# An unused tile of 96 bytes among the constants of a two-layer decoder trunk

## The chip, the cores and the metric

The kernel runs on one core of a Trainium2 chip. The metric is the device time of one execution in microseconds (us). A core has the engines TensorE (matrix products; PE in the profile, with its weight loads as PEld), VectorE (DVE), ScalarE (ACT), GpSimd (POOL) and SyncE (SP), which issues most of the transfers. The engines work on the on-chip memory of 128 partitions; an address here is a byte offset within a partition. TensorE writes its sums to a second memory, PSUM.

## What is computed

Two layers of a decoder over 256 tokens and 2048 features, in float32. Layer A's mixer is dilated attention, layer B's is a gated sum of compressed, selected-block and sliding-window attention. Cut to what matters:

```
h = x                                                   # (1, 256, 2048)
for i in range(2):
    hn = rmsnorm(h, attn_norm_g[i])
    if i == 0:
        h = h + dilated_mixture_attention(hn, a_w_in, a_w_out)
    else:
        shared = nsa_shared_kv(rmsnorm(h, kv_norm_g), w_kv_shared, ...)
        h = h + nsa_attention(hn, b_w_qg, b_w_out, *shared)
    hn = rmsnorm(h, mlp_norm_g[i])
    h = h + square(relu(hn @ mlp_w1[i])) @ mlp_w2[i]    # 2048 -> 8192 -> 2048
    gate = sigmoid(rmsnorm(h, ple_norm_g[i]) @ ple_w_gate[i])
    h = h + (p[i] @ ple_w_proj[i]) * gate
return rmsnorm(h, final_norm_g)
```

## The kernel before

Every matrix of weights is read once, in chunks of 128 x 1024 float32 (512 KB). `load` (L186) brings a chunk into a tile `raw`. ScalarE (`copy`, L198) rounds it into `whi`, a tile of type float32r, the type that TensorE multiplies at a higher rate than float32; VectorE (`sub`, L204) writes the rest, `raw - whi`, into `wlo`. Activations are split in the same way: a tile `xa` (or `h`, `oT`, `ko`, `pg`) holds the high part of 256 tokens in columns 0 to 255 and the low part in columns 256 to 511. A product is then the sum of three float32r products: high by high, high by low, low by high.

A matmul has a stationary operand of 128 x 128, which is loaded first as its weights, and a moving operand that streams past it.

- `mm_tiles` (L327, L329) does the products with the features in the partitions: 128 columns of `whi` as weights with all 512 columns of `xa` moving, then the same columns of `wlo` with the 256 columns of the high part. `quad` and `single` call it.
- `token_major` (L418, L419, L420) does the products with the tokens in the partitions: 128 columns of the activations as weights, and 512 columns of `whi` or `wlo` moving.
- The last chunk of the last gate (L382, L383, L384) uses 256 moving columns in all three products.
- Scores in layer A (L717, L718), the norms' sums (L237, L261) and the transposes (L491, L555, L746, L1180) are plain float32. The transposes have the constant `ident` as the moving operand; L261 has the constant `ones` as weights.

`Program.run` writes the order out: at each step it loads chunks up to 7 ahead, splits some, gives the active generators (the steps behind a product: sums, norms, softmax) one move each and lets TensorE work on one chunk. The work of the attention heads is hooked between chunks.

The tiles are given out pool by pool, in the order in which the pools are opened: `const`, `x`, `stat`, `tmp`, `xa`, `w`, and behind them pools that live for a stage (`A`, `h`, `O`, `B`, `C`, `S`). Within the constants the order is that of the program: `gains`, `ones`, `ident`, `ropeC`, `ropeS`, `pair`, `warm`. Each tile's size is rounded up to 32 bytes. `warm` has one float32 in each partition.

Of the kernel before, what the change touches and what calls it, by code (L numbers as in the profile page):

```python
# [10 lines left out]
F32 = mybir.dt.float32  # L11
# [4 lines left out]
P = 128  # L16
# [117 lines left out]
def kernel(ctx: ExitStack, tc: tile.TileContext, a: dict, out: bass.AP):  # L134
# [4 lines left out]
    const = ctx.enter_context(tc.tile_pool(name="const", bufs=1))  # L139
# [33 lines left out]
    ropeS = const.tile([32, T], F32, name="ropeS")  # L173
    pair = const.tile([P, 64], F32, name="pair")
    warm = const.tile([P, 1], F32, name="warm")
    nc.scalar.copy(warm, ones[:, :1])

    def load_x(j, half=None):
# [1155 lines left out]
```

## Time and profile before

| | |
|---|---|
| median of 3 runs | 2513.16 us (2512.55 to 2513.68) |
| profiled execution | 2514.11 us, its span 2511.3 us |
| mean granted TensorE clock | 0.999 |
| TensorE busy | 2500.4 us, 13497 matmuls |
| weight loads busy | 2156.5 us |
| VectorE busy | 1662.3 us |
| ScalarE busy | 1351.0 us |
| read from device memory | 461.65 MB, 185 GB/s over the span |

The span runs from the first to the last instruction of the profiled execution; the execution's own time also holds what lies around it. Busy time counts each instruction from its start to its end. Matmuls overlap, so that the duration of one (396 ns for 512 columns on L327) is longer than the distance from its start to the next one's start; the timeline shows the starts.

### The profile page before, as it was taken

To read this page: it belongs to the slowest core of one execution; us is meant where nothing else is said; L and a number is where in the kernel's file an instruction comes from. 1 tells how busy PE (TensorE), PEld (TensorE's weight loads), DVE (VectorE), ACT (ScalarE), POOL (GpSimd) and SP (SyncE) were. 2 spreads that over 40 slices of the span, in tenths; PEclk is the share of its full clock that TensorE was granted. 3 is DMA by queue.
4 is the path that set the end of the run, shared out by engine and by line. 5 is a ranking of instruction groups with operands and counts; after the bars stand their busy time and mean duration, and the time that the engine had idled before them with its cause. 6 is when DMAs were issued, how large, how long until landed. Compare 5 with 4: busy or idle time off the path is not lost.

```text
span 2511.3 us, 36082 instructions
## 1 busy us (share of the span) xinstructions
PE 2500.4 (100%) x13497; PEld 2156.5 (86%) x13497; DVE 1662.3 (66%) x2808; ACT 1351.0 (54%) x2168; POOL 10.4 (0%) x24
## 2 busy tenths in 40 slices
PE   9999999999999999999999999999999999999998
PEld 8888888888888888888888889888888888888887
DVE  7766677865465565566787989766546556556676
ACT  6444444554454453455564788755545445445455
POOL 0000000000000000000000000000000000000000
PEclk9999999999999999999999999999999999999999
DMA  7555545556555655555565753455555655665553
GB/s 272 172 179 178 175 161 181 173 188 193 193 188 193 191 192 193 192 192 185 186 195 189 243 163 121 141 191 190 192 192 188 193 192 192 193 192 190 182 189 121
DMA packets 130111, 466.10 MB, mean 186 GB/s; under 512 B 14608, under 2 KB 15888, under 8 KB 129936
## 3 DMA queue, kind: packets, MB, share of 16 engines
q1 hardware_dynamic: 129264, 462.68, 56.6%
q8 instruction: 105, 1.72, 0.3%
q0 software_dynamic: 528, 1.07, 0.2%
q14 instruction: 70, 0.57, 0.1%
q10 hardware_dynamic: 144, 0.07, 0.0%
HBM read 461.65 MB, written 2.10 MB: 185 GB/s over the span
## 4 chain that ended last, share of the span: by engine, by line
PE 99%; DVE 0%; DMA 0%; SPq 0%; ACT 0%; issue 0%; DVEq 0%
PE mm L327 22%; PE at L327 17%; PE mm L329 11%; PE at L329 9%; PE mm L418 6%; PE mm L420 6%; PE mm L419 6%; PE at L420 5%; PE at L418 5%; PE at L419 5%; PE at L1180 0%; PE at L718 0%; PE mm L1204 0%; PE mm L938 0%; PE mm L939 0%; DMA raw<-in_w_v 0%
## 5 line engine op out<-in xcount | busy, mean ns | idle before, releaser
L204 DVE TENSOR_TENSOR wlo<-raw,whi 128x1024 fp32r<-128x1024 f32 (+1 forms) x875 | 1065.7, 1219 | 634.3 <-PE at L420 131.5
L198 ACT CAST whi<-raw 128x1024 fp32r<-128x1024 f32 (+1 forms) x875 | 919.8, 1052 | 880.4 <-PE at L327 198.9
L327 PE MATMUL mm<-xa,whi 128*128 128x512 f32 x2176 | 756.4, 396 | 0.0
L329 PE MATMUL mm<-xa,wlo 128*128 128x256 f32 x2176 | 587.9, 278 | 0.0
L327 PE MATMUL at<-xa,whi 128*128 128x512 f32 x1648 | 573.7, 393 | 0.0
L327 PEld LDWEIGHTS mm<-xa,whi 128*128 128x128 f32 x2176 | 401.4, 188 | 85.1 <-issue 0.4
L329 PE MATMUL at<-xa,wlo 128*128 128x256 f32 x1648 | 458.5, 278 | 0.0
L329 PEld LDWEIGHTS mm<-xa,wlo 128*128 128x128 f32 x2176 | 409.4, 188 | 9.7
L327 PEld LDWEIGHTS at<-xa,whi 128*128 128x128 f32 x1648 | 308.7, 187 | 70.0
L329 PEld LDWEIGHTS at<-xa,wlo 128*128 128x128 f32 x1648 | 310.2, 188 | 0.1
L418 PE MATMUL at<-whi,h 128*128 128x512 f32 x512 | 199.5, 390 | 0.0
L418 PE MATMUL mm<-whi,h 128*128 128x512 f32 x512 | 199.4, 389 | 0.0
L419 PE MATMUL mm<-whi,h 128*128 128x512 f32 x512 | 199.2, 389 | 0.0
L420 PE MATMUL mm<-wlo,h 128*128 128x512 f32 x512 | 199.2, 389 | 0.0
L420 PE MATMUL at<-wlo,h 128*128 128x512 f32 x512 | 199.2, 389 | 0.0
L419 PE MATMUL at<-whi,h 128*128 128x512 f32 x512 | 199.2, 389 | 0.0
L420 PEld LDWEIGHTS at<-wlo,h 128*128 128x128 f32 x512 | 96.1, 188 | 20.0
L420 PEld LDWEIGHTS mm<-wlo,h 128*128 128x128 f32 x512 | 96.1, 188 | 20.0
L418 PEld LDWEIGHTS mm<-whi,h 128*128 128x128 f32 x512 | 96.1, 188 | 19.9
L419 PEld LDWEIGHTS at<-whi,h 128*128 128x128 f32 x512 | 96.1, 188 | 19.8
L418 PEld LDWEIGHTS at<-whi,h 128*128 128x128 f32 x512 | 96.1, 188 | 19.8
L419 PEld LDWEIGHTS mm<-whi,h 128*128 128x128 f32 x512 | 96.1, 188 | 19.6
(315 smaller groups left out, 2529.5 us busy)
## 6 DMA issues: line engine op xcount, KB each, us to landing
raw<-in_w SPq DMA_DIRECT2D x512, 512.0 KB, 3.6
raw<-in_w_qk SPq DMA_DIRECT2D x96, 512.0 KB, 3.5
raw<-in_w_gate SPq DMA_DIRECT2D x56, 512.0 KB, 4.0
raw<-in_w_kv SPq DMA_DIRECT2D x48, 512.0 KB, 4.3
raw<-in_w_v SPq DMA_DIRECT2D x46, 512.0 KB, 3.6
raw<-in_w_q SPq DMA_DIRECT2D x32, 512.0 KB, 4.4
raw<-in_w_oB SPq DMA_DIRECT2D x32, 512.0 KB, 3.5
raw<-in_w_oA SPq DMA_DIRECT2D x16, 512.0 KB, 3.5
```

Of the source, the lines that this page charges most:

```text
L198: nc.scalar.copy(hi[:, c], t[:, c])
L204: nc.vector.tensor_sub(lo[:, c], t[:, c], f32(hi)[:, c])
L327: nc.tensor.matmul(ps, hi[:, col:col + P], rhs, start=first, stop=False)
L329: nc.tensor.matmul(ps[:, :T], lo[:, col:col + P], rhs[:, :T], start=False, stop=last)
L418: nc.tensor.matmul(st[j], xh, wh, start=k == 0, stop=False)
L419: nc.tensor.matmul(st[j], xl, wh, start=False, stop=False)
L420: nc.tensor.matmul(st[j], xh, wl, start=False, stop=k == KT - 1)
```

## The change

One line is added among the constants. The tile has no name in the program, no instruction writes or reads it, and every pool opened after `const` begins 96 bytes further on.

```
     pair = const.tile([P, 64], F32, name="pair")
     warm = const.tile([P, 1], F32, name="warm")
+    const.tile([P, 24], F32, name="pad")
     nc.scalar.copy(warm, ones[:, :1])
```

More of the change, by code (lines that the diff above doesn't have):

```diff
@@ L175 @@
     warm = const.tile([P, 1], F32, name="warm")
+    const.tile([P, 24], F32, name="pad")
     nc.scalar.copy(warm, ones[:, :1])
```

## The prediction

> **What bounds the kernel now.** I read the page first: the busy times, then the chain that ended last, then the waits of TensorE.
>
> ```profile
> span 2511.3 us, 36082 instructions
> ...
> PE 2500.4 (100%) x13497; PEld 2156.5 (86%) x13497; DVE 1662.3 (66%) x2808; ACT 1351.0 (54%) x2168; POOL 10.4 (0%) x24
> ...
> PEclk9999999999999999999999999999999999999999
> ...
> PE 99%; DVE 0%; DMA 0%; SPq 0%; ACT 0%; issue 0%; DVEq 0%
> ```
>
> TensorE is the bound: 99% of the chain lies on it, the granted clock is full in every slice, and no other engine is busy for more than two thirds of the span. The longest rows of the view of waits for TensorE are these, and together they make under 2 us.
>
> ```profile
> PE mm L650 <- DVE ones L170: 1.1, 1, 1.1
> PE at L420 <- DVE wlo L204: 0.4, 1, 0.4
> ```
>
> So the end can move only if TensorE's own steps become shorter or longer. A matmul's duration in the groups is no step, since matmuls overlap; the step is the distance between two starts, which the timeline gives. In the MLP, where the factors alternate between 512 and 256 columns (L327, L329), the first and a later pair stand so:
>
> ```profile
> 899.83 0.39 PE L327 MATMUL mm<-xa,whi 128*128 128x512 f32 x1
> 900.07 0.27 PE L329 MATMUL mm<-xa,wlo 128*128 128x256 f32 x1
> ...
> 901.91 0.39 PE L327 MATMUL mm<-xa,whi 128*128 128x512 f32 x1
> ```
>
> Six pairs in 2.08 us are 347 ns for 768 columns. In the token-major half (L418 to L420), where every matmul has 512 columns, and at the last gate (L382 to L384), where every one has 256:
>
> ```profile
> 949.75 0.39 PE L418 MATMUL mm<-whi,h 128*128 128x512 f32 x1
> ...
> 952.92 0.39 PE L420 MATMUL mm<-wlo,h 128*128 128x512 f32 x1
> ```
> ```profile
> 2491.88 0.28 PE L382 MATMUL at<-xa,whi 128*128 128x256 f32 x1
> ...
> 2493.31 0.28 PE L382 MATMUL at<-xa,whi 128*128 128x256 f32 x1
> ```
>
> There are 14 steps in 3.17 us, 226.4 ns each, and 12 steps in 1.43 us, 119.2 ns each. The difference of 107 ns for 256 columns is 0.419 ns a column, which leaves 119.2 - 107.2 = 12 ns that do not grow with the columns. The pair agrees: 768 x 0.419 = 322 ns, and 25 ns are left for two matmuls. So each float32r matmul pays some 12.5 ns beside its columns. Plain float32 matmuls show no such term:
>
> ```profile
> 93.79 0.38 PE L717 MATMUL mm<-qk 128*128 128x128 f32 x2
> 94.01 0.60 PE L718 MATMUL at<-qk 128*128 128x256 f32 x2
> ...
> 95.10 0.38 PE L717 MATMUL mm<-qk 128*128 128x128 f32 x2
> ```
>
> From 93.79 to 95.10 us four matmuls of 128 columns and four of 256 ran: 1.31 us. Two of 128 took 0.22 us, 110 ns each, and the eight together leave (1.31 - 0.44) / 4 = 218 ns for 256 columns. Twice the columns take twice the time: the fixed part is nothing that two digits show, 2 ns at most, at half the rate (0.85 ns a column).
>
> **The change part by part.** It adds no instruction, no wait and no transfer; the tile is written and read by nobody, and 96 bytes more fit. What it moves is every tile allocated behind the constants. In the compiled program of before the constants run from byte 16512 (258 x 64) through sizes that are all multiples of 64 up to `warm` at 20352; `warm` holds 4 bytes and takes 32, so `x0` begins at 20384 = 318.5 x 64. The tiles behind it that TensorE reads, `xa`, `whi`, `wlo`, `h`, `ko`, `z`, `pt` among them, have sizes and slots that keep this: all begin 32 bytes past a multiple of 64. Only `ones`, `ident` and `pair` do not. With 96 bytes more `x0` begins at 20480 = 320 x 64, and the others at multiples of 64.
>
> No float32r operand of before begins at a multiple of 64, so the trace of before does not show what such a start costs, and I bound it. One bound is nothing gained, by the operands whose start does differ. The constants as weights and the shifted tiles as weights load equally long:
>
> ```profile
> L261 PEld LDWEIGHTS mm<-diag,ones x6: 188/188/189, 60.3 to 2422.1; 128*128 128x128 f32 x6
> ```
> ```profile
> L329 PEld LDWEIGHTS mm<-xa,wlo 128*128 128x128 f32 x2176 | 409.4, 188 | 9.7
> ```
>
> And `ident` as the moving operand, which is aligned, does not beat the 110 ns of `qk`, which is not: eight transposes of 128 columns make 0.87 us of the chain, 109 ns each.
>
> ```profile
> 1134.55 0.87 PE at L491 x8
> ```
>
> These are float32 matmuls at half the rate, where a late read has room to hide, so they do not settle it for float32r. The other bound is that all of the 12.5 ns is the price of the half-line start. I take 10.5 ns: the 12.5 ns less the 2 ns that the float32 rows allow. The reason is the contrast itself. The fixed term stands only where operands are read at the full rate, and has the size of a read: 12.5 ns are 12.5 / 0.419 = 30 columns or 120 bytes, about what a stream would fetch in vain at its two ends if it were cut at wider borders than its start. That is an inference, not something the trace shows. A loss has no reason on TensorE: all these tiles move by the same amount, so their starts relative to one another stay.
>
> By the Trainium skill, page "TensorE: Matmul & The Clock Gate", section "Back-to-back issue gap", the gap is N / 2.4 + 2.5 ns, 215.8 ns for 512 columns and 109.2 for 256. The trace's 226.4 and 119.2 differ from it by 10 ns. Were this rule reached the sum would come out within a few us of mine, as an estimate from that page.
>
> The counts come from the windows over the whole span for L327, L329, and L418 to L420, in that order:
>
> ```profile
> 0.00:2511.30 2511.30, 1486.26 (x4272) 793.66 (x4272) 1.00 0.57 186
> ...
> 0.00:2511.30 2511.30, 1171.05 (x4272) 804.01 (x4272) 1.00 0.57 186
> ...
> 0.00:2511.30 2511.30, 499.31 (x1280) 240.34 (x1280) 1.00 0.57 186
> ...
> 0.00:2511.30 2511.30, 498.26 (x1280) 240.37 (x1280) 1.00 0.57 186
> ...
> 0.00:2511.30 2511.30, 498.61 (x1280) 240.32 (x1280) 1.00 0.57 186
> ```
>
> They make 2 x 4272 + 3 x 1280 = 12,384 matmuls. Of the other 1113 about half are float32r (L771, L938, L1131, L1204 and the like), say 550, so 12,934. Times 10.5 ns that is 136 us.
>
> Not all of it arrives. In the MLP other engines have room, in layer B's heads hardly. The windows show both (columns: length, then PE, PEld, DVE, ACT, POOL busy, clock, DMA share, GB/s):
>
> ```profile
> 0.00:63.00 63.00, 61.54 (x319) 52.40 (x320) 44.32 (x67) 41.61 (x61) 0.20 (x4) 1.00 0.79 272
> ...
> 503.00:1100.00 597.00, 597.00 (x3092) 510.51 (x3091) 338.34 (x420) 296.21 (x408) 0.00 (x0) 1.00 0.59 191
> ...
> 1410.00:1440.00 30.00, 30.00 (x163) 24.89 (x162) 29.41 (x57) 25.76 (x49) 0.00 (x0) 1.00 0.81 260
> ...
> 1470.00:1500.00 30.00, 30.00 (x200) 26.98 (x199) 28.86 (x104) 25.97 (x84) 0.00 (x0) 1.00 0.38 118
> 1500.00:1550.00 50.00, 50.00 (x341) 46.05 (x340) 47.81 (x181) 42.83 (x134) 0.00 (x0) 1.00 0.39 121
> 1550.00:1600.00 50.00, 49.45 (x331) 45.04 (x330) 46.73 (x177) 42.34 (x129) 0.00 (x0) 1.00 0.40 127
> ```
>
> In the MLP VectorE is busy 338 of 597 us and the loads run at 191 GB/s where 272 were reached at the start, so a TensorE that is 5% faster is still the bound there. In the last four windows, 160 us, VectorE is busy 152.8 us. There 1035 matmuls would give 10.9 us, but VectorE leaves 7.2 us at the very most, of which I count half: 7 us are lost. In the first window the loads already run at their highest rate and 319 matmuls would give 3.3 us; I take off 1 us. 136 - 8 = 128 us. The profiled execution took 2514.1 us, so 2386, and the median of the runs lies 0.95 us below it: **2385 us**, 5.1% less.
>
> **The rivals.** *One read, not two.* If a start in mid-line costs one more read of 64 bytes, that is 16 columns, 16 x 0.419 = 6.7 ns, and the rest of the 12.5 ns stays. 12,934 x 6.7 = 87 us, less 4 in layer B's heads and at the start, gives 2430 us. For it speaks the unit of 64; against it that the measured term is nearer two such reads.
>
> *The fixed term belongs to float32r itself,* or the unused tile moves nothing: 2513 us. For it speak the equal loads of weights and the transposes above. By the Trainium skill, page "SBUF — State Buffer", section "Specifications (TRN2)", lines are 16 bytes long; 32 past 64 is a multiple of 16, so by that rule no start changes its line and the time stays. No row of before tests that at the full rate.
>
> *Slower: VectorE takes over in layer B's heads.* If its instructions suit the new starts worse and TensorE gains nothing, VectorE becomes the bound first in those 160 us, from 160 / 152.8, 4.7% longer instructions, on. At 10% longer it needs 168.1 us, 8 us more: 2521 us. Everywhere else its idle time covers that. Against it: relative starts stay the same, and its duration is in no row tied to a start.
>
> **How the numbers follow.** The full gain has a chance of 0.40, the one read 0.25, no change 0.26, the slower case 0.09. 0.2%, 5 us, is about what a measurement of this kernel can tell from no change. So faster 0.65, same 0.26, slower 0.09. If all 12.5 ns went, 162 us less 12 lost would give 2364 us, the low end; the high end, 2516, holds no change and leaves out most of the slower case.
>
> **What would show it.** Right: the steps of L418 to L420 fall from 226 to near 216 ns, those of L382 to L384 from 119 to near 109, the pair of L327 and L329 from 347 to near 325, and the float32 steps (L717, L718, L491) stay. New waits of TensorE on VectorE appear only near the heads of layer B. Steps of 220 and 113 ns mean the one read. Unchanged steps at a changed start mean that the term is float32r's own, and the prediction is wrong. Steps that shorten with L382 unchanged would mean that weight loads, not moving reads, set the short matmuls.

## The result, and the profile after

The kernel with the tile takes 2519.83 us (median of 11 runs, 2519.51 to 2520.83), the kernel before 2513.16 us (11 runs): ratio 1.0026, 95% interval 1.0017 to 1.0035. It is slower by 6.7 us, just beyond what a measurement of this kernel tells from no change. 5.1% faster was forecast. All lines of the code behind the added one are one higher.

The page of the kernel after: TensorE is still the bound and busy for 6.9 us longer, with the same number of matmuls; VectorE and ScalarE are busy as long as before.

```profile
span 2518.9 us, 36082 instructions
...
PE 2507.3 (100%) x13497; PEld 2158.8 (86%) x13497; DVE 1662.0 (66%) x2808; ACT 1351.4 (54%) x2168; POOL 10.4 (0%) x24
...
L328 PE MATMUL at<-xa,whi 128*128 128x512 f32 x1648 | 579.4, 397 | 0.0
```

The group that grew most is L328 into `at`, 573.7 before. The waits of TensorE are as short as they were (view of waits, the two longest):

```profile
PE mm L651 <- DVE ones L170: 1.1, 1, 1.1
PE at L421 <- DVE wlo L205: 0.4, 1, 0.4
```

The steps that were to fall did not. Token-major matmuls and the last gate's, timeline after, columns as in the prediction:

```profile
949.52 0.39 PE L419 MATMUL mm<-whi,h 128*128 128x512 f32 x1
...
952.92 0.39 PE L419 MATMUL mm<-whi,h 128*128 128x512 f32 x1
```
```profile
2498.66 0.28 PE L383 MATMUL at<-xa,whi 128*128 128x256 f32 x1
...
2499.38 0.28 PE L383 MATMUL at<-xa,whi 128*128 128x256 f32 x1
```

15 steps in 3.40 us are 226.7 ns, and 6 steps in 0.72 us are 120 ns, as before. The time went elsewhere. The chain in order of time has the same groups of matmuls in both kernels, and their starts date the loss. Before:

```profile
1202.74 0.87 PE mm L491 x8
...
1457.01 3.73 PE mm L1081 x16
...
2333.35 0.87 PE at L491 x8
...
2497.79 1.75 PE mm L555 x16
```

After:

```profile
1203.17 0.87 PE mm L492 x8
...
1460.62 3.71 PE mm L1082 x16
...
2338.45 0.88 PE at L492 x8
...
2504.58 1.75 PE mm L556 x16
```

The lag is 0.4 us at the end of the first MLP, 3.6 us behind the first gate and the shared keys, 5.1 us in the second MLP and 6.8 us at the end. It grows only where the 512/256 pairs run one to one. Ahead of the first MLP, at 503 us, the kernel after is even 0.8 us ahead, so the first MLP itself costs 1.3 us. The first MLP shows how, before and after, each from a time of 540 us:

```profile
539.88 0.39 PE L327 MATMUL mm<-xa,whi 128*128 128x512 f32 x1
...
541.96 0.39 PE L327 MATMUL mm<-xa,whi 128*128 128x512 f32 x1
```
```profile
539.93 0.40 PE L328 MATMUL mm<-xa,whi 128*128 128x512 f32 x1
540.16 0.28 PE L330 MATMUL mm<-xa,wlo 128*128 128x256 f32 x1
540.28 0.40 PE L328 MATMUL mm<-xa,whi 128*128 128x512 f32 x1
540.52 0.28 PE L330 MATMUL mm<-xa,wlo 128*128 128x256 f32 x1
540.64 0.40 PE L328 MATMUL mm<-xa,whi 128*128 128x512 f32 x1
540.88 0.28 PE L330 MATMUL mm<-xa,wlo 128*128 128x256 f32 x1
540.99 0.40 PE L328 MATMUL mm<-xa,whi 128*128 128x512 f32 x1
...
542.05 0.40 PE L328 MATMUL mm<-xa,whi 128*128 128x512 f32 x1
```

Six pairs take 2.08 us before and 2.12 us after. TensorE goes in a rhythm that it keeps: 230 + 117 ns for each pair before, and after a figure of three pairs, 233 + 117, 241 + 120, 236 + 113 ns, which is 353.3 ns a pair instead of 346.7. The slow figure is not new; before has it too, for 127 pairs of layer A's output projection among others, where six pairs take 2.12 us:

```profile
469.71 0.40 PE L327 MATMUL mm<-oT,whi 128*128 128x512 f32 x1
...
471.83 0.40 PE L327 MATMUL mm<-oT,whi 128*128 128x512 f32 x1
```

Counting by the starts every pair that stands in three successive pairs of 1055 ns or more (1040 is the fast rhythm), before has 592 slow pairs and after 1691; how the ends of stretches are counted moves each of these by up to some 40. 1099 pairs x 6.67 ns = 7.3 us. Summed over the whole traces, the steps inside the pairs are 7.3 us longer and all other steps together 0.5 us shorter, which leaves the 6.8 us. 1035 of the slow pairs lie in five stretches that before has not: 191, 263, 191, 191 and 199 pairs from 512, 1224, 1324, 1715 and 2427 us on.

### The profile page after: what moved, and what is told of

The parts are those of the page before. It is cut to its first block, busy times and chain, and to the rows that moved or that the text cites. A ratio compares the mean times of both kernels' runs of the same rounds, so it can differ in the third digit from the quotient of the medians.

```text
span 2518.9 us, 36082 instructions
## 1 busy us (share of the span) xinstructions
PE 2507.3 (100%) x13497; PEld 2158.8 (86%) x13497; DVE 1662.0 (66%) x2808; ACT 1351.4 (54%) x2168; POOL 10.4 (0%) x24
## 4 chain that ended last, share of the span: by engine, by line
PE 99%; DVE 0%; DMA 0%; SPq 0%; ACT 0%; issue 0%; DVEq 0%
PE mm L328 22%; PE at L328 17%; PE mm L330 11%; PE at L330 9%; PE mm L420 6%; PE mm L421 6%; PE mm L419 6%; PE at L421 5%; PE at L419 5%; PE at L420 5%; PE at L1181 0%; PE at L719 0%; PE mm L1205 0%; PE mm L939 0%; PE mm L940 0%; DMA raw<-in_w_v 0%
## 5 line engine op out<-in xcount | busy, mean ns | idle before, releaser
L328 PE MATMUL mm<-xa,whi 128*128 128x512 f32 x2176 | 757.5, 396 | 0.0
L328 PE MATMUL at<-xa,whi 128*128 128x512 f32 x1648 | 579.4, 397 | 0.0
L328 PEld LDWEIGHTS mm<-xa,whi 128*128 128x128 f32 x2176 | 401.5, 188 | 85.5 <-issue 0.4
L328 PEld LDWEIGHTS at<-xa,whi 128*128 128x128 f32 x1648 | 309.4, 188 | 74.5
L419 PE MATMUL at<-whi,h 128*128 128x512 f32 x512 | 199.5, 390 | 0.0
L419 PE MATMUL mm<-whi,h 128*128 128x512 f32 x512 | 199.4, 389 | 0.0
L420 PE MATMUL mm<-whi,h 128*128 128x512 f32 x512 | 199.3, 389 | 0.0
L420 PE MATMUL at<-whi,h 128*128 128x512 f32 x512 | 199.2, 389 | 0.0
L419 PEld LDWEIGHTS mm<-whi,h 128*128 128x128 f32 x512 | 96.1, 188 | 20.0
L420 PEld LDWEIGHTS at<-whi,h 128*128 128x128 f32 x512 | 96.1, 188 | 19.9
L419 PEld LDWEIGHTS at<-whi,h 128*128 128x128 f32 x512 | 96.1, 188 | 19.8
L420 PEld LDWEIGHTS mm<-whi,h 128*128 128x128 f32 x512 | 96.1, 188 | 19.6
```

The source lines that it names most:

```text
L328: nc.tensor.matmul(ps, hi[:, col:col + P], rhs, start=first, stop=False)
L419: nc.tensor.matmul(st[j], xh, wh, start=k == 0, stop=False)
L420: nc.tensor.matmul(st[j], xl, wh, start=False, stop=False)
```

## The experiments

Two things were asked: what sets the rhythm, and whose the fixed 12.5 ns are. The tables give slow pairs in the profiled execution, the median, and the ratio to the kernel before on the same chip with its interval.

**How far everything moves.** The edit is the size of the unused tile, `[P, 8]`, `[P, 16]`, `[P, 32]`, `[P, 56]`, `[P, 64]`, `[P, 88]`.

```
    const.tile([P, 8], F32, name="pad")      # pad32; the others alike
```

pad32: 

> The unused tile has 32 bytes, so x0 begins at 20416, a multiple of 64 but not of 128. Theory A (what counts is the start within 64 bytes): the same slow rhythm of the 512/256 pairs as with 96 bytes, 236+113, 233+117, 241+120 ns, in some 1690 pairs instead of 590, and about 2520 us. Rival B (any move of the addresses throws the dice anew): some other set of slow stretches, anywhere from 2511 to 2522 us. Rival C (the start within 128 bytes counts): not like 96 bytes; nearer 2513 us.

pad64: 

> The unused tile has 64 bytes: everything moves, but x0 begins at 20448, 32 past a multiple of 64 as before. Theory A: stretch by stretch the rhythm of the kernel before, some 590 slow pairs, within 0.05% of 2513 us. Rival B: another set of slow stretches. Rival C (128): differs from before, since 20448 is 96 past a multiple of 128 and not 32.

pad128: 

> The unused tile has 128 bytes: x0 begins at 20512, again 32 past a multiple of 128. Theory F (the place of the streamed tiles within 128 bytes decides, 32 and 64 past one are good, 0 and 96 are bad): the same list of slow stretches as the kernel before, some 592 slow pairs, and 2513 us. Rival B (every move throws the dice anew): a list that is neither that of before nor that of 96 bytes.

pad224: 

> The unused tile has 224 bytes: x0 begins at 20608, a multiple of 128 as with 96 bytes, and everything lies 128 bytes further on than there. Theory F (the place within 128 bytes): the slow stretches of the kernel with 96 bytes, some 1690 slow pairs, 2520 us. Rival B (every move throws the dice anew): even chances of 2513 us.

pad256: 

> The unused tile has 256 bytes. Theory J (the place of the tiles within 256 bytes picks the rhythm: whi's first tile at 160, 192, 32, 64 or 128 past a multiple of 256 is good, at 224 and 0 bad): the slow stretches of the kernel before, the same in layer A's heads too, 592 slow pairs and 2513 us. Rival B (every move throws the dice anew): another list.

pad352: 

> The unused tile has 352 bytes, 256 more than the change's. Theory J: the long slow stretches behind the four spreads, some 1690 slow pairs, 2520 us, the same list as with 96 bytes. Rival B: most moves so far were good ones, so 2513 to 2515 us.

| kernel | bytes | slow pairs | the five long stretches | us | ratio |
|---|---|---|---|---|---|
| before | 0 | 592 | none | 2513.16 | 1 |
| pad32 | 32 | 745 | none | 2513.69 | 1.0002 (0.9992 to 1.0011) |
| pad64 | 64 | 1709 | all | 2520.05 | 1.0028 (1.0017 to 1.0039) |
| after | 96 | 1691 | all | 2519.83 | 1.0026 (1.0017 to 1.0035) |
| pad128 | 128 | 636 | none | 2513.08 | 0.9998 (0.9989 to 1.0007) |
| pad224 | 224 | 897 | none | 2514.73 | 1.0007 (0.9997 to 1.0016) |
| pad256 | 256 | 850 | none | 2513.60 | 1.0000 (0.9991 to 1.0010) |
| pad352 | 352 | 1670 | all | 2519.95 | 1.0027 (1.0016 to 1.0037) |

A multiple of 64 is not it: 32 bytes and 96 both give one, and only one is slow; 64 bytes give none and is slow (theory A falls). A period of 128 fell with 224 bytes (theory F). 256 bytes more repeat both kernels in the long stretches and in the time. Two such agreements alone could be chance, since five of the eight kernels have no long stretch; but pad352 has the smaller stretches of layer A's heads, too, where after has them, and pad64 has others besides. The smaller slow stretches of layer A's heads in before do not repeat in pad256. That profiled execution of pad256 took 2515.64 us where the median is 2513.60, so those seem to vary between executions. That the period is 256 rests on two pairs of kernels.

**diag alone.** The moving operand of the norm's spread (L261), behind which the long stretches set in:

```
-                self.diag = stat.tile([P, T], F32, tag="diag", name="diag", bufs=1)
+                self.diag = stat.tile([P, T + 16], F32, tag="diag", name="diag", bufs=1)[:, 8:8 + T]
```

after_diag: 

> The kernel with the 96 bytes, with diag alone (the moving operand of L261/L262) begun 32 bytes past a multiple of 64 again; every other tile keeps its multiple of 64. Theory D (the step of the norm's spread matmul decides how the pairs behind it fall in): the start of the first pair comes 425 ns after the second record again instead of 420, the long slow stretches behind the four spreads at 512, 1223, 1715 and 2427 us go, about 850 pairs x 6.67 ns = 5.6 us less, some 2514 us. Rival E (the start of the streamed operands themselves decides): still 2520 us.

before_diag: 

> The kernel before, with diag alone begun at a multiple of 64; every other tile stays 32 past one. Theory D: 420 ns behind the spread, and slow pairs behind the four spreads as with the 96 bytes: some 5 us more, 2518 us. Rival E: 2513 us, no new slow stretch.

| kernel | slow pairs | us | ratio |
|---|---|---|---|
| after_diag | 541 | 2512.36 | 0.9997 (0.9987 to 1.0006) |
| before_diag | 1572 | 2519.23 | 1.0024 (1.0014 to 1.0034) |

Both times came as theory D had them, but the step it named did not: behind the spread after_diag was to show 425 ns again, and shows 418 or 419. The edit also moves all tiles behind `diag` by 64 bytes, which the expectations overlooked: `whi` lies then 160 bytes further on than before in after_diag, and 64 in before_diag, just as in pad64. pad64 has its `diag` at another start and the same stretches, and besides them the one from 1324 us, which before_diag lacks. So these two do not show that `diag` counts. They count as shifts of 160 (good) and 64 (bad).

What theory D looked at does tell the rhythms apart. In the traces of the ten kernels of these two tables, five spreads each stand where a long stretch can follow. The step from the first matmul behind the spread to the second takes 420 ns ahead of each of the 19 long stretches (five each in after, pad64 and pad352, four in before_diag), and 417 to 419 or 425 ns in the 31 places where none follows; before_diag has 418 ns at 1324 us. (These are read in ns from the starts in the traces.) pad256 repeats the steps of before one by one, 425, 425, 417, 425 and 425 ns, which no other of the ten does; that, too, speaks for a period of 256. So this one step already tells the rhythm, as long as all these tiles move together: w_stage below has 420 ns or 421 at some spreads and no long stretch. What sets the step is not shown.

**The rhythm without a move.** The kernel after, with the first chunk of five quads (one in each MLP, one in each gate, one of the keys) in the order `whi`, `whi`, `wlo`, `wlo`:

```
-                     run=2 if b and not q else 1)
+                     run=2 if q == (not b) else 1)
-                     lambda f, ps, q=q: gate_done(4 * q + f, ps), hooks)
+                     lambda f, ps, q=q: gate_done(4 * q + f, ps), hooks, run=2 if q == 1 else 1)
-        quad(lambda c: a["w_kv"][i * 8 + c], KT, x_kv, done, hooks)      # key_quad
+        quad(lambda c: a["w_kv"][i * 8 + c], KT, x_kv, done, hooks, run=1 + which)
```

> The kernel with the 96 bytes; nothing moved in memory. In the first chunk of four quads (q = 1 of the first MLP block, q = 1 of the gate, the quad kw) the matmuls go two whi, two wlo instead of one and one, as other quads of the kernel do. Theory G (a rhythm that a stretch falls into and keeps; the start of the tiles only picks it): behind these chunks the pairs take 347 ns instead of 353, some 850 of the 1691 slow pairs go, 5.7 us less, about 2514 us. Rival E (the start of the operands makes each of these matmuls longer): the pairs stay at 353 ns and the time at 2520 us.

2516.75 us, 1.0014 (1.0004 to 1.0024), 1215 slow pairs. 476 pairs fewer than after, x 6.67 ns = 3.2 us; 3.1 us were gained. Both gates' long stretches are gone with every tile where it was, and with 420 ns behind the spread as in after: the pairs between the spread and the changed chunk are still slow, those behind it fast; the timeline of after_run in the first gate has three pairs in 1.04 us:

```profile
1239.62 0.40 PE L328 MATMUL at<-xa,whi 128*128 128x512 f32 x1
...
1240.66 0.39 PE L328 MATMUL at<-xa,whi 128*128 128x512 f32 x1
```

The two MLPs and the keys stayed slow, so half of the expected gain came: the rhythm can be left, but this order does not always leave it. The slow pairs are not what a matmul at that start takes by itself.

**One operand against the other.** 96 or 64 unused bytes ahead of one group of tiles, and 32 or 64 behind it, so that the rest keeps its place within 128 (w_stage has none behind).

```
+    xap.tile([P, 24], F32, tag="pad", name="pad", bufs=1)      # xa_only
+    wpool.tile([P, 8], F32, tag="pad", name="padw", bufs=1)
```

xa_only: 

> The split activations xa alone begin at a multiple of 128 (two unused tiles, 96 bytes ahead of xa and 32 behind, so that whi, wlo and all behind them stay 32 past one). If the moving operand's start decides: long slow stretches behind the spreads as in the changed kernel, some 1500 to 1700 slow pairs, 2519 to 2520 us. If the start of the weights decides: 2513 us.

w_only: 

> The chunk tiles raw, whi and wlo alone begin at a multiple of 128 (96 unused bytes ahead of them, 32 behind, so that h, oT, ko and the other stage tiles stay 32 past one, and xa stays too). If the start of the weights decides: 2519 to 2520 us with the long slow stretches. If the moving operand's start decides: 2513 us. If only the two together decide, both this kernel and the one with xa alone stay at 2513 us.

w_stage: 

> The 96 unused bytes stand between xa and the chunk tiles: raw, whi, wlo and all stage tiles (h, oT, ko) begin at multiples of 64 as in the changed kernel, xa, x and the small tiles stay 32 past one. Theory H (what counts is the start of the moving operand against that of the weights, and more than either against a fixed line): the 512/256 pairs stay at 347 ns with no slow stretch, as with the chunk tiles alone moved; the token-major matmuls with h as weights go back from 233 to 227 ns, since h and whi have the same offset again; those with xa as weights stay at 233. Together 2513 to 2516 us. Rival A (each operand's own start counts): 233 ns stay for whi on h, and 2530 us or more.

xa_64: 

> xa alone moved by 64 bytes, so that it begins half a line of 128 away from whi and wlo. Theory H: the step of the pairs and of the token-major matmuls with xa as weights changes, those with h as weights stay at 227 ns. Which way is open: with 96 bytes (the same as 32 the other way) the cost was 21 us; if one half of a 128-byte line is served while the other is read, this is the best distance of all and the time falls below 2513 us; if any distance costs, it is 2525 to 2540 us.

w_64: 

> raw, whi and wlo alone moved by 64 bytes against xa and against h, oT, ko. Theory H: as with xa alone moved by 64 for the pairs, and in addition the 3072 token-major matmuls with h as weights change their step from 227 ns. If half a line apart is best, below 2513 us, down to 2490; if any distance costs, 2530 to 2550 us.

| kernel | moved | pairs, ns | L418 to L420 on h, ns | us | ratio |
|---|---|---|---|---|---|
| xa_only | xa by 96 | 353 in four of five | 227 | 2534.74 | 1.0085 (1.0070 to 1.0100) |
| w_only | raw, whi, wlo by 96 | 347, none slow | 233 | 2534.79 | 1.0083 (1.0068 to 1.0098) |
| w_stage | these and the stage tiles by 96 | 347, 260 slow | 227 | 2515.76 | 1.0011 (1.0001 to 1.0020) |
| xa_64 | xa by 64 | 353 | 227 | 2534.66 | 1.0085 (1.0070 to 1.0100) |
| w_64 | raw, whi, wlo by 64 | 353 | 233 | 2554.81 | 1.0165 (1.0148 to 1.0182) |

xa_only and w_only came outside all that was expected of them, 2513 to 2520 us. The distance between the two operands' starts counts, and more than the change itself (theory H). With `h` and `whi` at equal places within 128 bytes a step is 227 ns, 32 or 64 apart 233. The distance within 128 bytes is not all of it: with `xa` as weights and `whi` 64 apart, in xa_64, the mean step is 228.5 to 230.5 ns. In w_only every token-major step is longer, 13 steps in 3.03 us, 233 ns each (timeline of w_only):

```profile
949.81 0.40 PE L423 MATMUL mm<-wlo,h 128*128 128x512 f32 x1
...
952.84 0.40 PE L421 MATMUL mm<-whi,h 128*128 128x512 f32 x1
```

w_stage restores that distance and falls back to 2516 us. Nothing here beats the kernel before: the pairs never go under 347 ns, so all that a better rhythm could still bring is 592 x 6.67 ns = 3.9 us, 0.16%.

**The fixed term.** scan gives `whi` and `wlo` another start every 16 chunks; ld64 loads 64 columns of weights for L419 instead of 128; measure puts rows of equal matmuls ahead of the kernel.

```
+        o = STARTS[n // 16 % len(STARTS)]               # scan; lo alike
-        hi = wpool.tile([P, CH], ...)
+        hi = wpool.tile([P, CH + 32], ...)[:, o:o + CH]
```
```
-                        nc.tensor.matmul(st[j], xl, wh, start=False, stop=False)      # ld64
+                        nc.tensor.matmul(st[j][:64], xl[:, :64], wh, start=False, stop=False)
```
```
+        for _ in range(24):                             # measure: 13 such rows
+            nc.tensor.matmul(ps[:, :512], wt, mv[:, 1:513], start=True, stop=True)
```

scan: 

> The kernel before with whi and wlo given 128 bytes more, and the start within them changing every 16 chunks: 0, 4, 8, 16, 24, 32, 48, 64, 96 bytes (one buffer of es less, for space); the steps of TensorE are grouped by the distance from the weights' start to the moving operand's, within 128 bytes. Theory H (the distance counts): for h as weights 227 ns at distance 0 as before, 233 at 32, 64, 96 as seen; if what collides are lines of 16 bytes, 4 and 8 are like 0 and 16 to 48 like 32; if lines of 64, 16 and 24 are like 0. Rival K (a start off a multiple of 32 costs by itself): 4, 8, 16, 24 and 48 are longer than all others. Were the 12.5 ns a collision that some distance avoids, one of them would show 216 ns.

2544.38 us (one run). No distance gave 216 ns. With `h` as weights the means are 235 to 237 ns at 4 bytes, 233 at 8, 231 at 16, 233 at 24 and 32, 231 to 232 at 48, 231 at 64, 234 at 96, rhythms mixed; no chunk with `h` as weights fell on 0.

ld64: 

> In the token-major matmuls the low part of the activations is loaded as 64 columns of weights instead of 128, so that half of that product's tokens lack this correction; the second of each three matmuls then waits for a weight load half as long. Theory L (the fixed 12.5 ns belongs to a weight load): the step into or out of L419 falls from 227 ns by 6 to 12 ns, up to 1024 + 256 matmuls, 8 to 15 us less in all. Rival M (it belongs to the moving operand or to float32r itself): all three steps stay 227 ns and the time stays within noise.

2535.77 us (one run): theory L's gain did not come. The load took 134 ns instead of 188, and no line's mean step fell; all three lines' steps came to 230 ns in a mixed rhythm (224 to 236), and the kernel became 22 us slower.

measure: 

> The kernel before with rows of 24 equal matmuls put ahead of it (some 70 us more), all operands begun 32 bytes past a multiple of 128: bf16 and float32r of 512 and 256 columns, float32r of 384, and float32r of 512 with the moving operand begun 4, 8, 16, 32, 64 and 96 bytes further on. Theory N (the 12.5 ns belong to float32r): bf16 takes 216 ns for 512 columns and 109 for 256, float32r 227, 173 and 120 at distance 0. Rival O (they belong to any matmul at one column a cycle that loads its own weights): bf16 takes 227 and 120 as well. Distances: by the kernels with tiles moved, 32, 64 and 96 bytes take some 233 ns; if lines of 16 bytes count, 4 and 8 bytes take no more than 227, if any distance counts, 233 or more.

The timeline of measure. Among float32r rows one begins where the one before it ended, so the difference of two starts is the length of a row. Where the type changes it is not (the last bf16 step reads 28 ns), so bf16 is read from the single steps inside its rows (L661 bf16 of 512 columns; L665 to L675 float32r at distances of 4, 8, 16, 32, 64, 96 bytes; L677 and L679 of 256 and 384 columns at 0; L681 bf16 of 256; L683 float32r of 512 at 0):

```profile
13.79 5.13 PE L661 MATMUL mm<-mb,wb 128*128 128x512 bf16 x23
18.57 5.82 PE L663 MATMUL mm<-mv,wt 128*128 128x512 f32 x24
24.22 5.84 PE L665 MATMUL mm<-mv,wt 128*128 128x512 f32 x24
29.90 5.75 PE L667 MATMUL mm<-mv,wt 128*128 128x512 f32 x24
35.49 5.72 PE L669 MATMUL mm<-mv,wt 128*128 128x512 f32 x24
41.05 5.76 PE L671 MATMUL mm<-mv,wt 128*128 128x512 f32 x24
46.65 5.66 PE L673 MATMUL mm<-mv,wt 128*128 128x512 f32 x24
52.14 5.77 PE L675 MATMUL mm<-mv,wt 128*128 128x512 f32 x24
57.75 3.03 PE L677 MATMUL mm<-mv,wt 128*128 128x256 f32 x24
60.62 4.33 PE L679 MATMUL mm<-mv,wt 128*128 128x384 f32 x24
64.79 2.79 PE L681 MATMUL mm<-mb,wb 128*128 128x256 bf16 x24
67.34 5.72 PE L683 MATMUL mm<-mv,wt 128*128 128x512 f32 x24
```

float32r takes 119.6 ns for 256 columns (2.87 / 24), 173.8 for 384, and in the settled part of L683, its last 17 steps, 226.7 for 512: 13.3 ns beside the columns. bf16 steps are 216 ns and 109 ns: 2.5 ns beside the columns, with operands begun at the same place as float32r's. That is what theory N said. It does not yet part float32r's moving operand from its weight load, since bf16's load is shorter too, 98 ns against 188:

```profile
L661 PEld LDWEIGHTS <-wb x24: 96/98/100, 13.6 to 18.3; 128*128 128x128 bf16 x24
L663 PEld LDWEIGHTS mm<-mv,wt x24: 187/188/190, 18.5 to 23.8; 128*128 128x128 f32 x24
```

Against the load speaks ld64, but there only one load in three was shorter, and by 54 ns. The distances cost 236.7, 232.9, 231.7, 233.3, 228.8 and 233.8 ns. Only 0 gives 227, and behind a bf16 row it takes seven uneven steps to get there. At 64 bytes it is 228.8 ns here, 231 in scan and 233 in w_64, so the distance alone does not say how long a step is.

## Why the prediction was wrong

The step that failed is "I take 10.5 ns", the share of the fixed term that was laid to the start in mid-line. It measured 0: 226.7 and 120 ns with every float32r operand on a multiple of 64. The term itself was read rightly, 12.5 ns against 13.3 in measure, and so was the contrast with plain float32. The inference from the contrast was not. It allowed two readings, that the start costs or that float32r costs, and the size in bytes was taken for evidence of the first. The runs speak for the second: without the start in mid-line the float32r steps stayed, and bf16 at the same start as float32r does not pay the term. Whether it comes with the type, with reading four bytes a column at the full rate or with float32r's longer weight load (188 ns against 98) stays open. The rival that the term is float32r's own was right about the steps, with a chance of 0.26, but not about the time.

"A loss has no reason on TensorE" failed too. The starts relative to one another do stay within what moved, yet the stretches of 512/256 pairs fell into the slow rhythm, 1099 pairs more. That rhythm stood in the trace of before, in 592 pairs; the prediction averaged one good stretch and took it for all. The slower case that it priced, VectorE in layer B's heads, did not happen: the lag grows by 0.1 us there. The high end of 2516 us left out a case of 2520.

The terms that hang on the gain, 136 us and the 8 us taken off it, were not tested. The Trainium skill's rule for an isolated matmul in "TensorE: Matmul & The Clock Gate", section "Back-to-back issue gap", agrees with bf16 (215.8 and 109.2 ns against 216 and 109) and not with float32r (227 and 120); here the measurement decides. The Trainium skill's rule of 16-byte lines in "SBUF — State Buffer", section "Specifications (TRN2)", gave no change for this edit; the time changed, and in measure distances of 16, 32 and 96 bytes, all multiples of it, cost 5 to 7 ns.

Shown: the loss is slow pairs; the same tiles can run in either rhythm (after_run); moving the tiles changes which one a stretch falls into, and the step behind the spread tells which. Likely, by two pairs of kernels: the same outcome 256 bytes further on. Not shown: through which operand the place does so, and what in TensorE holds the rhythm.

## What to carry to other kernels

Where TensorE is the bound, read its steps from the starts of matmuls, over all stretches of one shape: two stretches of the same shape that differ by a few ns a pair are a rhythm, and edits that do no work can flip it. Compare a suspected cost with another type at the same place before laying it to the place. Here moving one of two groups of tiles that stream against each other cost 0.8 to 1.7%, and moving all of them at most 0.3%.

## What the runs showed of the hardware

A float32r matmul costs 13.3 ns beside its columns at the best distance tried (120, 173.8, 226.7 ns for 256, 384, 512 columns), bf16 2.5 ns (109 and 216 ns for 256 and 512). The distance of the moving operand's start from the weights' start changed the step of 512 columns in measure from 227 to between 229 and 237 ns, with 4 bytes the worst. Alternating 512 and 256 columns settled into periodic figures of 346.7 or 353.3 ns a pair and kept them for up to 263 pairs. With one weight load in three shorter (134 instead of 188 ns), the mean token-major steps were longer (230 instead of 227 ns), in one run.
